# Plain products for the first pair of n-tiles, a casting load for the second weight quad, and new places for the w_down pieces in a fused GeGLU MLP

## Chip, cores and metric

One core of one Trainium2 chip. The metric is device time in microseconds (us) of one launch, median over runs of the same kernel. Engines in the profile: PE is TensorE's matmuls, PEld its weight loads, DVE VectorE, ACT ScalarE, POOL GpSimd, SP the engine that issues plain DMA; a name with a q behind it (SPq, POOLq) is its queue of DMA issues.

## The reference

```python
x: (8, 1024, 1024) fp32;  w_gate, w_up: (1024, 4096);  w_down: (4096, 1024)
gate = x @ w_gate
up   = x @ w_up
gate = 0.5 * gate * (1 + tanh(sqrt(2/pi) * (gate + 0.044715 * gate**3)))
out  = (gate * up) @ w_down
```

## The kernel before

The kernel works through 8192 tokens in eight passes of 1024, all operands in fp16, with accumulation in fp32. In each pass "gate_up" makes h and "down" multiplies it by w_down. Gate_up of passes 0 to 2 takes 16 pairs of 128-wide n-tiles (gate and up weights of both), each pair by a seven-product (Strassen-Winograd) scheme: 14 product steps of 4 matmuls of 512 columns. Operands of five of the products are sums of token blocks (`sum_x`) or of weight blocks (`sum_w`), made by VectorE. Two pairs share a weight quad: 512 columns of both weights, in one of two ring slots. Quads come by a load from GpSimd's queue that casts fp32 to fp16. Pass 0 also has to fetch and transpose its own tokens, and to make w_down's operands, which all later passes read back.

```python
def x0_rest():                      # second half of tokens and of the first weight columns: pair 0, after step 4
    for g in range(G):
        x0_cast(1, g)               # DVE, fp32 -> fp16
    for kh in range(2):
        for w in range(2):
            cast_first(w, kh, slice(256, 512))      # ACT
    used = [ps_free[g] for g in range(G)]
    for g in range(G):
        x0_transpose(1, g)          # PE, then copies by DVE and ACT
    write_banks(used)               # identity matmuls
    ...                             # sum_w and sum_x in turns

# start of the kernel: transposes of the first token half, then
write_banks(range(8))               # eight identity matmuls, 512 columns
for kh in range(2):
    for w in range(2):
        cast_first(w, kh, slice(0, 256))

# in gate_up_one, pass 0
first = p == 0 and i == 0
if first:
    at(4, x0_rest)
for u in range(8 if q == 0 else 0):         # second quad: staged in fp32, cast by ACT in eight pieces
    s = (5, 8, 11, 14, 16, 18, 20, 22)[u]
    if s // 14 == e:
        k = s % 14 + 1
        at(k, cast_stage, 8 + u)
        at(k, load_stage, 8 + u + 4)
...
if e == 1:
    at(13, load_raw, p, q + 2)              # next quad by casting DMA, step 13 of an odd pair
for n in range(4):                          # four batches of w_down
    s0 = 36 * n + 34                        # product step, counted through pass 0
    for ds, f, a in (
        (0, wd_load, (n, 0)), (2, wd_load, (n, 1)), (4, wd_load, (n, 2)), (6, wd_load, (n, 3)),
        (14, wd_sums, (0,)), (15, wd_sums, (1,)), (16, wd_sums, (2,)), (17, wd_sums, (3,)),
        (19, wd_store, (n,)),
    ):
        pr, k = divmod(s0 + ds - 1, 14)
        if pr == i:
            at(k + 1, f, *a)                # wd_load: casting DMA; wd_sums: DVE; wd_store: SP

# in down(p): transposes of the next pass's tokens by DMA
if v == (2 if p < FAST - 1 else 0):
    transpose_x(p + 1)
```

## Time and profile before

| | |
|---|---|
| median of 3 runs | 2315.16 us (2313.58 to 2316.32) |
| span of the profiled run | 2316.7 us (its time, 2318.57, lies above all three) |
| TensorE busy | 2282.1 us, 99% |
| VectorE, ScalarE, GpSimd busy | 58%, 42%, 29% |

A timeline line reads: start, length in us, engine, kernel line, operation, what it writes and reads, how many in a row, and in brackets how long the engine had been idle before it and what ended that. In the view of waits: total us, how often, the longest. The prediction shows the lines.

To compare kernels stage by stage I also counted matmul records. No record seems to be missing in these traces (14,668 before, 14,696 after: 28 more, as the code says), so the n-th matmul from the end is the same one in each. That gives the start of each pair and of each down to 0.01 us. Pairs are numbered from 0, so the second pair is pair 1. An undisturbed pair takes 12.09 us, an undisturbed down 96.69 us.

### The profile page before, as it was taken

To read this page: it belongs to the slowest core of one execution; us is meant where nothing else is said; L and a number is where in the kernel's file an instruction comes from. 1 tells how busy PE (TensorE), PEld (TensorE's weight loads), DVE (VectorE), ACT (ScalarE), POOL (GpSimd) and SP (SyncE) were. 2 spreads that over 40 slices of the span, in tenths; PEclk is the share of its full clock that TensorE was granted. 3 is DMA by queue.
4 is the path that set the end of the run, shared out by engine and by line. 5 is a ranking of instruction groups with operands and counts; after the bars stand their busy time and mean duration, and the time that the engine had idled before them with its cause. 6 is when DMAs were issued, how large, how long until landed. Compare 5 with 4: busy or idle time off the path is not lost.

```text
span 2316.7 us, 38115 instructions
## 1 busy us (share of the span) xinstructions
PE 2282.1 (99%) x14668; PEld 1435.2 (62%) x14668; DVE 1350.2 (58%) x1951; ACT 969.9 (42%) x1874; POOL 671.3 (29%) x817
## 2 busy tenths in 40 slices
PE   6989999999999999999999999999999999999999
PEld 3434444444444444888458884688747886488854
DVE  4655547884377862666536673466734667356650
ACT  5434116552155521565125551355414553055520
POOL 1333003330033300454105450145402543034520
PEclk9999999999999999999999999999999999999999
DMA  6978988889799886898779886798857988588762
GB/s 220 188 139 174 254 229 204 203 233 287 188 214 225 210 292 214 272 321 276 219 239 296 300 275 203 257 312 279 278 192 265 316 280 263 194 278 276 268 215 109
DMA packets 258149, 559.28 MB, mean 241 GB/s; under 512 B 74864, under 2 KB 132208, under 8 KB 243824
## 3 DMA queue, kind: packets, MB, share of 16 engines
q1 hardware_dynamic: 204992, 483.46, 61.9%
q0 software_dynamic: 50800, 69.21, 18.1%
q10 hardware_dynamic: 2176, 4.19, 0.5%
q8 instruction: 114, 1.87, 0.3%
q14 instruction: 67, 0.55, 0.1%
HBM read 512.75 MB, written 113.25 MB: 270 GB/s over the span
## 4 chain that ended last, share of the span: by engine, by line
PE 91%; DMA 3%; DVE 2%; SPq 2%; ACT 1%; issue 1%; POOL 0%; ACTq 0%; DVEq 0%; POOLq 0%
PE ps L713 39%; PE ps L825 32%; PE ps L496 20%; SPq L177 1%; DMA ring<-in_w_up_dram 1%; DVE ring L295 1%; DVE tmp L515 1%; DVE x_sums L200 1%; DMA h_a<-in_w_up_dram 0%; DMA ring<-wd_ops 0%; DMA h_a<-in_w_gate_dram 0%; DVE h_a L533 0%; DMA h_s<-in_w_down_dram 0%; ACT ring L260 0%; ACT tmp L507 0%
## 5 line engine op out<-in xcount | busy, mean ns | idle before, releaser
L713 PEld LDWEIGHTS <-ring 128*128 128x128 f16 x8320 | 814.1, 98 | 95.2
L690 POOL TENSOR_TENSOR h_a<-tmp 128x256 f16<-128x256 f32 x640 | 465.3, 747 | 927.4 <-ACT tmp L678 893.5
L713 PE MATMUL ps<-x_sums,ring 128*128 128x256 f16 x5760 | 655.8, 273 | 0.0
L825 PE MATMUL ps<-ring,h_a 128*128 128x512 f16 x2944 | 638.3, 379 | 1.7 <-DMA ring<-wd_ops 1.7
L675 DVE TENSOR_TENSOR tmp<-tmp,ps 128x512 f32<-128x512 f32 x640 | 413.9, 683 | 219.4 <-PE ps L713 166.2
L825 PEld LDWEIGHTS <-h_a 128*128 128x128 f16 x3072 | 300.5, 98 | 363.3 <-DVE tmp L768 2.2
L496 PEld LDWEIGHTS <-ring 128*128 128x128 f16 x2688 | 264.2, 98 | 339.8 <-issue 25.8
L660 ACT COPY tmp<-ps 128x512 f32<-128x512 f32 x520 | 304.4, 585 | 203.4 <-PE ps L713 125.7
L496 PE MATMUL ps<-x_sums,ring 128*128 128x512 f16 x1536 | 355.0, 384 | 13.2 <-DVE h_a L533 5.9
L678 ACT ACTIVATE tmp<-tmp 128x256 f32<-128x256 f32 x640 | 263.7, 417 | 173.3 <-DVE tmp L673 80.5
L764 ACT ACTIVATE tmp<-ps 128x512 f32<-128x512 f32 x128 | 76.4, 597 | 589.1 <-PE ps L825 589.1
L713 PE MATMUL ps<-x_b,ring 128*128 128x256 f16 x2560 | 305.6, 273 | 0.0
L522 POOL TENSOR_TENSOR h_a<-tmp 128x512 f16<-128x512 f32 x96 | 147.6, 1538 | 431.4 <-ACT tmp L520 350.5
L496 PE MATMUL ps<-x_b,ring 128*128 128x512 f16 x1152 | 265.0, 379 | 1.7 <-ACT ps L512 0.9
L673 DVE TENSOR_TENSOR tmp<-ps,tmp 128x512 f32<-128x512 f32 x240 | 165.5, 689 | 152.2 <-ACT tmp L660 104.8
L768 DVE SCALAR_TENSOR_TENSOR tmp<-ps,tmp 128x512 f32<-128x512 f32 x64 | 44.2, 691 | 305.3 <-ACT tmp L764 260.3
L515 DVE TENSOR_TENSOR tmp<-ps,tmp 128x512 f32<-128x512 f32 x192 | 129.6, 684 | 133.7 <-ACT tmp L507 131.2
L507 ACT COPY tmp<-ps 128x512 f32<-128x512 f32 x192 | 112.4, 586 | 97.2 <-PE ps L496 89.5
L772 DVE TENSOR_TENSOR h_a<-h_a,h_a 128x2048 f16<-128x2048 f16 x96 | 111.2, 1215 | 58.3 <-PE ps L825 58.3
L295 DVE TENSOR_TENSOR ring<-ring 128x1024 f16<-128x1024 f16 x192 | 136.0, 722 | 11.1 <-DMA ring<-in_w_up_dram 7.0
L520 ACT ACTIVATE tmp<-tmp 128x512 f32<-128x512 f32 x96 | 60.1, 626 | 157.9 <-DVE tmp L515 157.9
L825 PE MATMUL ps<-ring,h_s 128*128 128x512 f16 x480 | 104.9, 379 | 0.0
(63 smaller groups left out, 784.8 us busy)
## 6 DMA issues: line engine op xcount, KB each, us to landing
ring<-w_ops SPq DMA_DIRECT2D x480, 512.0 KB, 4.6
ring<-wd_ops SPq DMA_DIRECT2D x105, 1024.0 KB, 5.2
out_dram<-tmp SPq DMA_DIRECT2D x128, 256.0 KB, 3.0
w_ops<-x_sums SPq DMA_DIRECT2D x110, 256.0 KB, 6.2
ring<-in_w_gate_dram POOLq DMA_DIRECT2D x22, 1024.0 KB, 10.0
ring<-in_w_up_dram POOLq DMA_DIRECT2D x22, 1024.0 KB, 17.6
w_ops<-h_s SPq DMA_DIRECT2D x82, 256.0 KB, 4.8
x_half<-in_x_dram POOLq DMA_DIRECT2D x7, 2048.0 KB, 15.5
```

The costliest lines, as they stand in the source:

```text
L295: nc.vector.tensor_tensor(o, a, b, op)
L496: nc.tensor.matmul(ps(b, w), lhs[:, k], rhs[:, k, :], start=(first and k == 0), stop=(k == KH - 1), skip_group_check=True,)
L507: nc.scalar.copy(tl((n, w)), ps("a", w))
L515: nc.vector.tensor_tensor(o, ps("b", w), o, ADD)
L522: nc.gpsimd.tensor_tensor(hq[TO[n]][:, i, :], tmp[:, t[n, 1]], tmp[:, t[n, 0]], MUL)
L660: nc.scalar.copy(tmp[:, t[o[1]]], ps_all[:, bank[o[2]]])
L673: nc.vector.tensor_tensor(d, b, a, SUB)
L675: nc.vector.tensor_tensor(d, a, b, ADD if o[4] == "add" else SUB)
L678: nc.scalar.activation(d, d, GELU, scale=GSC)
L690: nc.gpsimd.tensor_tensor(h, tmp[:, t[o[1]], MQ : 2 * MQ], g, MUL)
L713: nc.tensor.matmul(ps_all[:, bank[c], w * MQ : (w + 1) * MQ], lhs[:, w, k], rhs[:, k], start=(first and w == 0 and k == 0), stop=(k == KH ...
L825: nc.tensor.matmul(ps_all[:, bank[b, g]], lhs[:, j, g * P : (g + 1) * P], dc[:, n, :], start=(first and j == 0), stop=(j == NP - 1), skip_ ...
```

## The change

Intent: start the array earlier. Pair 0 is done by eight plain products, ordered so that the first half of tokens and the first weight columns are enough for the first 32 matmuls, and half of K for the first 16 of them. The second quad comes by casting DMA, released once half of the second-column casts are done (a one-column GpSimd copy into `mark` waits for the cast). The w_down batches get places such that no quad is issued between their pieces. The removal of the staging helpers, and of `write_banks` and `x0_rest`, is cut here.

```diff
+            if p == 0 and i == 0:
+                first_pair()
+                continue
             if p == 0:
-                for u in range(8 if q == 0 else 0):
-                    ...                                  # eight cast_stage / load_stage
                 if e == 1:
                     at(13, load_raw, p, q + 2)
...
-                    s0 = 36 * n + 34
+                    s0 = 28 * n + 59
...
-                        (14, wd_sums, (0,)), (15, wd_sums, (1,)),
-                        (16, wd_sums, (2,)), (17, wd_sums, (3,)), (19, wd_store, (n,)),
+                        (16, wd_sums, (0,)), (17, wd_sums, (1,)),
+                        (18, wd_sums, (2,)), (19, wd_sums, (3,)), (21, wd_store, (n,)),
...
-            pair(p, i, extra, SEQ0 if first else SEQ, AFTER0 if first else AFTER1)
+            second = p == 0 and i == 1
+            pair(p, i, extra, SEQ0 if second else SEQ, AFTER0 if second else AFTER1)
...
+    def first_pair():
+        ...                     # products(mh, kh, c): tokens mh, K half kh, token columns c; outputs: gelu, mul
+        for g in range(G):
+            x0_cast(0, g)
+        for g in range(G):
+            x0_transpose(0, g)
+        for kh in range(2):
+            for w in range(2):
+                cast_first(w, kh, slice(0, 256))
+        take(0)
+        for kh in range(2):
+            products(0, kh, slice(0, MH))
+        for g in range(2):
+            x0_cast(1, g)
+        for g in range(2):
+            x0_transpose(1, g)
+        outputs(0, 0)
+        outputs(0, 1)
+        for g in range(2, G):
+            x0_cast(1, g)
+        take(1)
+        for kh in range(2):
+            products(1, kh, slice(0, MQ))
+        for g in range(2, G):
+            x0_transpose(1, g)
+        ...                     # order of free PSUM banks
+        for n, (kh, w) in enumerate(((0, 0), (0, 1), (1, 0), (1, 1))):
+            cast_first(w, kh, slice(256, 512))
+            if n == 1:
+                nc.gpsimd.tensor_copy(mark, raw(0, 0)[:, w, kh * KH, 256:257])
+                load_raw(0, 1)
+        for kh in range(2):
+            products(1, kh, slice(MQ, MH))
+        sum_x(1)
+        ...                     # sums of the second pair, outputs(1, 0), outputs(1, 1)
```

More of the change, by code (lines that the diff above doesn't have):

```diff
@@ L143 @@
     identity = const.tile([P, P], FP16, name="identity")
+    mark = const.tile([P, 1], FP16, name="mark")
     xq = {
@@ L239, in ssum @@
         return rg[:, o : o + 4096].rearrange("p (s w k n) -> p s w k n", s=4, w=2, k=KH)
-    def staging(u):
-        o = 8192 + (u % 4) * 2048
-        return xc[:, o : o + 2048].bitcast(FP32).rearrange("p (k n) -> p k n", k=2)
-    def eighth(u):
-        q, e = divmod(u, 8)
-        k, w = divmod(e, 2)
-        return q, w, slice(2 * k, 2 * k + 2)
-    def load_stage(u):
-        q, w, k = eighth(u)
-        if q == 1:
-            nc.scalar.dma_start(
-                out=staging(u), in_=w_v[w][:, k, q * 512 : (q + 1) * 512]
-            )
-    def cast_stage(u):
-        q, w, k = eighth(u)
-        nc.scalar.copy(raw(0, q)[:, w, k], staging(u))
     def staging0(w, kh):
@@ L553, in at @@
                 extra[k].append(lambda: f(*a))
-            first = p == 0 and i == 0
-            if first:
-                at(4, x0_rest)
+            if p == 0 and i == 0:
+                first_pair()
+                continue
             if p == 0:
-                for u in range(8 if q == 0 else 0):
-                    s = (5, 8, 11, 14, 16, 18, 20, 22)[u]
-                    if s // 14 == e:
-                        k = s % 14 + 1
-                        at(k, cast_stage, 8 + u)
-                        at(k, load_stage, 8 + u + 4)
-                if first:
-                    for u in range(8, 12):
-                        at(5, load_stage, u)
                 if e == 1:
@@ L593, in gate_up_one @@
                 at(13, load_raw, p, q + 2)
-            ks = (6, 8, 10, 12) if first else (3, 5, 7, 9) if e == 0 else (11, 12, 13, 14)
+            ks = (3, 5, 7, 9) if e == 0 else (11, 12, 13, 14)
             for n, k in enumerate(ks):
@@ L898, in down, with products, outputs, take @@
         order[0] = order[0][2:] + order[0][:2]
-    def write_banks(banks):
-        for b in banks:
-            nc.tensor.matmul(
-                ps_all[:, b], identity, x0_f16[:, 0, 0:MH],
-                start=True, stop=True, skip_group_check=True,
-            )
-    def x0_rest():
+    def first_pair():
+        bank = {}
+        def products(mh, kh, c):
+            for w in range(2):
+                for j in range(2):
+                    for k in range(KH):
+                        nc.tensor.matmul(
+                            ps_all[:, bank[mh, j, w], c],
+                            raw(0, 0)[:, w, kh * KH + k, j * P : (j + 1) * P],
+                            xq[f"b{kh + 1}{mh + 1}"][:, k, c],
+                            start=(kh == 0 and k == 0 and c.start == 0),
+                            stop=(kh == 1 and k == KH - 1),
+                            skip_group_check=True,
+                        )
+        def outputs(mh, j):
+            t = tmp_free.popleft()
+            g, u = bank[mh, j, 0], bank[mh, j, 1]
+            nc.scalar.activation(tmp[:, t], ps_all[:, g], GELU, scale=GSC)
+            nc.vector.tensor_tensor(
+                hq[f"a{mh + 1}{j + 1}"][:, 0, :], ps_all[:, u], tmp[:, t], MUL
+            )
+            tmp_free.append(t)
+            ps_free.extend((g, u))
+        def take(mh):
+            for j in range(2):
+                for w in range(2):
+                    bank[mh, j, w] = ps_free.popleft()
@@ L909, in x0_rest @@
         for g in range(G):
-            x0_cast(1, g)
+            x0_cast(0, g)
+        for g in range(G):
+            x0_transpose(0, g)
         for kh in range(2):
             for w in range(2):
-                cast_first(w, kh, slice(256, 512))
-        used = [ps_free[g] for g in range(G)]
-        for g in range(G):
-            x0_transpose(1, g)
-        write_banks(used)
-        for k in range(2):
-            sum_w(0, 0, k)
-            sum_x(k + 1)
-        for k in range(2):
-            sum_w(0, 0, k + 2)
-            sum_x(k + 3)
+                cast_first(w, kh, slice(0, 256))
@@ new lines, in first_pair @@
+        take(0)
[4 more added lines that the diff above has]
+        for g in range(2):
+            x0_transpose(1, g)
+        outputs(0, 0)
[7 more added lines that the diff above has]
+            x0_transpose(1, g)
+        b = list(ps_free)
+        ps_free.clear()
@@ new lines, in first_pair @@
+        ps_free.extend((b[2], b[0], b[3], b[1]))
+        for n, (kh, w) in enumerate(((0, 0), (0, 1), (1, 0), (1, 1))):
[6 more added lines that the diff above has]
+        sum_x(1)
+        sum_w(0, 1, 0)
+        sum_w(0, 1, 1)
+        sum_x(2)
+        outputs(1, 0)
+        outputs(1, 1)
@@ L925 @@
+        sum_x(3)
+        sum_w(0, 1, 2)
+        sum_w(0, 1, 3)
+        sum_x(4)
     for g in range(G):
@@ L933 @@
                 x0_load(1, g)
-    for g in range(G):
-        x0_cast(0, g)
-    for g in range(G):
-        x0_transpose(0, g)
-    write_banks(range(8))
-    for kh in range(2):
-        for w in range(2):
-            cast_first(w, kh, slice(0, 256))
     for p in range(NPASS):
```

## The prediction

> **What bounds the kernel now.** I read the page first, then all waits of TensorE, then the chain that ended last, then the instructions in order of time at the two places where TensorE stood still. The page:
>
> ```profile
> span 2316.7 us, 38115 instructions
> PE 2282.1 (99%) x14668; PEld 1435.2 (62%) x14668; DVE 1350.2 (58%) x1951; ACT 969.9 (42%) x1874; POOL 671.3 (29%) x817
> PE   6989999999999999999999999999999999999999
> ```
>
> TensorE is the bound: 99% busy, with its only weak slices at the start (57.9 us each). At most 2316.7 - 2282.1 = 34.6 us of idle can be won without removing matmuls. All waits of TensorE over the whole run:
>
> ```profile
> PE ps L903 <- ACT x_b L229: 7.5, 1, 7.5
> PE ps L226 <- DVE h_a L219: 6.8, 6, 5.1
> PE ps L496 <- DVE h_a L533: 5.9, 1, 5.9
> PE ps L496 <- ACT ps L512: 3.2, 5, 1.1
> PE ps L496 <- ACT tmp L507: 2.3, 2, 1.4
> ```
>
> The first, second and fifth, and the first idle of the fourth (0.9), lie in the first pair of n-tiles (before 43 us). The third is one hole at 143 us. The change aims at exactly these. The hole, in the chain that ended last (start, us, what):
>
> ```profile
> 130.02 7.54 DMA h_s<-in_w_down_dram
> 137.56 8.53 issue
> 146.09 0.13 DVE h_s L356
> ```
>
> and in order of time on VectorE and TensorE:
>
> ```profile
> 130.02 0.59 POOL L338 DMA_DIRECT2D h_s<-in_w_down_dram  x1
> 146.09 0.69 DVE L356 TENSOR_TENSOR h_s<-h_s 128x1024 f16<-128x1024 f16 x1 [8.54 <-issue]
> 148.64 1.87 PE L496 MATMUL ps<-x_sums,ring 128*128 128x512 f16 x4 [5.87 <-DVE h_a L533]
> 151.58 6.63 PE L496 MATMUL ps<-x_sums,ring 128*128 128x512 f16 x20 [1.08 <-ACT ps L512]
> ```
>
> The last w_down piece of the third batch is issued at 130.02, just behind the two casting transfers of a weight quad (128.26 and 129.15). It takes 16.0 us to land, where its three predecessors took 4 to 5. VectorE, in order, sits on the sum that needs it; the products behind it wait; PSUM isn't freed; TensorE stops for 5.87 + 1.08 us. Afterwards 24 matmuls take 1.87 + 6.63 = 8.50 us; at the usual 0.216 us each they take 5.18. Together 10.3 us. Check: the same matmul group of two successive pairs starts at 123.61, 135.70 and then 158.05; a pair is 12.09, so 22.35 is 10.26 late.
>
> The start, in order of time:
>
> ```profile
> 9.98 3.27 PE L903 MATMUL ps<-h_a,identity 128*128 128x512 f16 x8
> 13.09 1.89 PE L496 MATMUL ps<-x_b,ring 128*128 128x512 f16 x8
> 26.66 1.04 ACT L273 CAST ring<-h_a 128x1024 f16<-128x1024 f32 x1 [1.68 <-DMA h_a<-in_w_up_dram]
> 28.24 2.05 PE L903 MATMUL ps<-h_a,identity 128*128 128x512 f16 x4 [7.45 <-ACT x_b L229]
> 53.33 4.48 PE L496 MATMUL ps<-x_b,ring 128*128 128x512 f16 x20
> ```
>
> After 16 matmuls of the first pair (P1, P2) nothing more can be done until the second half of tokens is transposed, which on ScalarE stands behind casts of the second weight columns; the last waits for its load until 26.66. Then half-speed matmuls and ScalarE's eight second-quad casts. Counting 56 matmuls per pair, the second pair begins at 43.07 and the third at 53.33 + 12 x 0.216 = 55.92. With 14 pairs at 12.10 (169.3) and the 10.3 hole the pass should end at 235.5; the chain puts down's first matmul at 235.91. So the sum closes.
>
> **What the Trainium skill says.** (1) "TensorE: Matmul & The Clock Gate", Part 1: an idle array runs at half clock, and gets the full one after about 3.4 us of sustained work in a free-running window. The trace agrees: matmuls of 0.427 us in the 4.8 us after 28.24 and until 156.1, at a granted clock of 0.50; 0.216 otherwise. (2) "DMA: Bandwidth & Descriptors", SWDGE vs HWDGE: a load that casts can only be issued from GpSimd, and only one such queue is allocated. The trace fits: a small casting load behind a quad waits for it. (3) Same page, Anatomy of one DMA: about 2 us + bytes/436e3. For 2 MiB read that is 6.8 us; the trace has 8.5 and 13.2 for the gate and up halves issued at 54.40 and 55.48, and I use those. (4) "PSUM — Partial Sum Buffer", The four PSUM rules: bits that say "written" are set by TensorE only. I read the identity matmuls as setting them before ScalarE seeds a bank; plain products set them too. No run shows this yet.
>
> **The change part by part.**
>
> *a. Plain products for pair 0.* Removed: 56 half-output products, 12 identity matmuls (3.27 + 2.05 us, but partly beside waits). Added: 2 token halves x 2 K halves x 2 weights x 2 tiles x 4 = 32 matmuls of 512 columns and 64 of 256, i.e. 64 full ones: 8 more than before, 1.73 us. What is gained is order: 32 of them need only the first tokens and first weight columns. Working forward with durations of the trace:
> - The first cast ends at 12.3 (11.26 + 1.04), the fourth at 15.3. TensorE starts at 12.4, cold, as nothing warms it. I take 5 us at 0.427 (12 matmuls) and 20 at 0.216: to 21.8. The loads don't bind it.
> - 16 transposes (1.06) to 22.9, their ScalarE copies to 23.5; 32 matmuls of 256 columns (3.5) to 27.0.
> - ScalarE: table load 1.28, two GELUs to 25.9; VectorE: two h products to 26.6, then the last two token casts to 27.9. So transposes end at 28.4, copies at 29.0.
> - ScalarE's four second-column casts (all landed by 26.6) run 29.0 to 33.0. The last 32 short matmuls (3.5) read the same tiles; a load into the other columns of a staging tile already waits for the former one in this trace (12.78, for the landing at 12.77), so I let the casts pace them: to 33.9.
> - The second pair, in the order P1, P2, P5...: 33.9 + 12.1 = 46.0. VectorE supplies its operands from 33.0: two weight sums (0.6), one x sum (1.2), two products (1.3), x sum (1.2), two weight sums, x sum (1.2): t2 at 35.5, t3 at 38.0, t4 at 40.4; the matmuls that need them come at about 38, 41 and 42.5. It fits.
>
> *b. Second quad by casting DMA.* Removed: eight ScalarE casts (8 x 1.04 us) and 4 MB of loads from ScalarE's queue. Added: one tiny GpSimd copy and the quad's two loads, held until the second cast (31.0). Issues at 31.3 and 32.3; landing + 8.5 and + 13.2: 39.8 and 45.5. The sums for pair 2 need both, and stand on VectorE after step 10 of pair 1, at about 43. They hold it to 46; the third pair's third product group wants its operand at 48.6 and gets it at about 48.5. I allow 0.5: third pair at an effective 46.5.
> Gain of a and b: 55.92 + 0.2 (a wait on VectorE at 58.87) - 46.5 = 9.6 us.
>
> *c. w_down pieces ahead of quads.* Each batch now has its four pieces at steps 3 to 9 of an even pair, sums at steps 5 to 8 of the odd one, and the next quad at its step 13; no quad is issued between pieces. The first batch of before had nearly this place: issued at 60.5 and 66.7 behind a quad of 54.4, sums waited 3.3 and 0.6 us and ran at 72.54 and 73.82, with no wait of TensorE. From the pair's start (55.92) that is 16.6 and 17.9; the new slots are at 12.1 + 4 x 0.864 = 15.6. VectorE would wait some 1.6 us four times, over before the accumulation in step 13. I credit the whole hole: 10.3 us.
>
> Sum: 9.6 + 10.3 = 19.9. The forward pass leaves out semaphore delays and smaller waits, and these only add; 1.7 us for them. 2315.2 - 18.2 = **2297 us**. Passes 1 to 7 have no changed instruction.
>
> **Rivals.**
> - *The quad's load becomes the new wait.* It starts at 31 instead of the staged loads' 26.7, and its second half has no reserve. Against: the queue is empty then. If up takes 17.6 us (median of the run), pair 2 starts 4 to 5 us later: 2301.
> - *The cold clock eats the start.* No identity matmuls warm the array. For: the windows are free-running, so 3.4 to 6.8 us cold; short pauses at 23, 27 and 28 could fail a window. Costs 1 to 4 us: up to 2301.
> - *The hole moves.* Every batch now lands 16 to 18 us after its pair's start, behind a quad, and four of them could each cost TensorE 1 to 2 us: 2301 to 2305. The first batch of before speaks against it.
> - *Start hidden by a later limit.* If down of pass 0 waited on transfers bound to absolute time, gains would be returned. Its only DMA wait is 1.7 us, and its transfers are issued relative to matmuls; unlikely. All lost: 2315.
> - *Better than thought:* a warm array at once and no pacing: 2291.
>
> **Range and chances.** Start gain 5 to 12, hole 7 to 10.5 with both rarely at an end: 2290 to 2304. Over 2% faster needs 2269, a gain of 46 us, more than all idle time (34.6): 1%. 2% slower needs a new hole of 46 us: 1%.
>
> **What would show it.** The waits of TensorE lose the 7.5 on L229's copies and the 5.9 on the h product; no hole near 130 to 150. First plain matmuls near 12.4 at 0.427 us, half speed for 3 to 7 us; second pair at 34, third near 46, down's first matmul near 217 (235.9 before). The quad's up half lands near 45. Wrong would be: third pair after 50, a wait on h products in an odd pair, or a wait in down that was not there.

## The result

The changed kernel: 2300.39 us median of 4 runs (2299.53 to 2304.98); the kernel before in the same comparison 2315.59 us (2313.58 to 2316.32). Ratio 0.994, 95% interval 0.9923 to 0.9957. A ratio here is the mean time of one kernel's runs over that of the other's runs of the same rounds, so it isn't quite the ratio of the medians quoted. The gain is 15.2 us where 18.2 were predicted; the time lies in the predicted range. Its size is less sure than that looks: when the changed kernel was timed again (experiment 11) the ratio was 0.9922, some 18 us. The profiled run happens to be the slowest of the four; a likely reason is told below.

The page of the changed kernel, the lines that answer to those of before:

```profile
span 2303.0 us, 38141 instructions
PE 2277.2 (99%) x14696; PEld 1436.5 (62%) x14696; DVE 1348.0 (59%) x1945; ACT 958.4 (42%) x1860; POOL 670.1 (29%) x818
PE   7999999999999999999999999999999999999999
```

Only the first slice is weak now. All waits of TensorE over the run:

```profile
PE ps L476 <- DVE tmp L495: 7.1, 5, 2.4
PE ps L227 <- DVE h_a L220: 6.8, 5, 5.1
PE ps L795 <- DMA ring<-wd_ops: 3.9, 1, 3.9
PE ps L879 <- ACT ring L253: 2.3, 1, 2.3
PE ps L879 <- DVE x_b L229: 1.1, 2, 0.6
PE ps L476 <- ACT ps L492: 0.5, 1, 0.5
```

The two big ones are gone: 7.5 us on ScalarE's token copies and 5.9 on the h product. The 6.8 us on token casts, of which 5.1 lie before the first token has landed, are as before, though the prediction lists them among what the change aims at. New is 7.1 us, in five pieces, on VectorE's accumulations (line 495), and the wait for a w_down chunk in down has grown from 1.7 to 3.9. The start, in order of time on several engines:

```profile
12.38 9.95 PE L879 MATMUL ps<-x_b,ring 128*128 128x512 f16 x32 [2.32 <-ACT ring L253]
...
28.31 1.22 PE L227 MATMUL ps<-identity,h_a 128*128 128x128 f16 x16 [0.85 <-DVE h_a L220]
...
32.68 1.08 POOL L260 DMA_DIRECT2D ring<-in_w_gate_dram  x1
...
33.53 1.89 PE L476 MATMUL ps<-x_b,ring 128*128 128x512 f16 x8
33.76 0.90 POOL L260 DMA_DIRECT2D ring<-in_w_up_dram  x1
...
46.69 0.69 DVE L275 TENSOR_TENSOR ring<-ring 128x1024 f16<-128x1024 f16 x1 [2.36 <-DMA ring<-in_w_up_dram]
...
50.97 4.48 PE L476 MATMUL ps<-x_sums,ring 128*128 128x512 f16 x20 [1.92 <-DVE tmp L495]
```

TensorE starts its first product at 12.38 and the second pair at 33.53 (43.07 before). But the second quad is released only at 32.68, its up half lands at 46.7, VectorE stands 2.36 us waiting for it, and TensorE then 1.92 us in the third pair. The fourth batch of w_down pieces, on VectorE, GpSimd and TensorE:

```profile
165.49 0.69 DVE L334 TENSOR_TENSOR h_s<-h_s 128x1024 f16<-128x1024 f16 x1 [5.84 <-DMA h_s<-in_w_down_dram]
...
170.07 1.26 POOL L502 TENSOR_TENSOR h_a<-tmp 128x512 f16<-128x512 f32 x1 [8.31 <-DVE tmp L495]
...
174.89 1.45 PE L476 MATMUL ps<-x_sums,ring 128*128 128x512 f16 x6 [1.29 <-DVE tmp L495]
```

VectorE waits 5.84 us for pieces. GpSimd waits for VectorE's accumulation, and only after that, at 171.29, issues the next quad. 9 us after VectorE's wait TensorE waits 1.29 for VectorE. In down of pass 0, the queue of plain DMA and TensorE:

```profile
250.59 30.89 SPq L178 DMA_TRANSPOSE x_b<-x_half  x4
...
293.81 6.38 PE L795 MATMUL ps<-ring,h_a 128*128 128x512 f16 x21 [3.93 <-DMA ring<-wd_ops]
```

Four DMA transposes hold that queue for 30.89 us (28.41 before). The load of the sixth product's chunk stands behind them, and after 3.93 us of idle the array also runs at half clock for a while (matmuls 0.43 us apart from 294.7 to 298.1).

The stages, worked out from the starts of matmuls in the two profiles (us):

| stage | before | after | difference |
|---|---|---|---|
| up to the second pair | 43.07 | 33.53 | -9.54 |
| second pair | 12.85 | 12.74 | -0.11 |
| third pair | 12.44 | 14.20 | +1.76 |
| pairs 3 to 7 | 60.43 | 60.43 | 0.00 |
| pairs 8 and 9 | 34.44 | 24.35 | -10.09 |
| pairs 10 to 13 | 48.35 | 51.22 | +2.87 |
| pairs 14 and 15 | 24.17 | 24.17 | 0.00 |
| down, pass 0 | 98.57 | 102.47 | +3.90 |
| gate_up of passes 1 and 2 | 393.44 | 390.95 | -2.49 |
| all that is later, to the last matmul | 1584.91 | 1584.90 | -0.01 |

Up to down the change is worth 15.11 us in this pair of profiles. What comes later isn't shown to be its effect: gate_up of passes 1 and 2 varies by 1.6 and 2.5 us between the profiles of any of these kernels, and down of pass 0 by more. The 15.11 us have a spread too. Three profiles with the old start and places (before, before again, experiment 9) start down at 234.80 to 235.75, three with the new ones (changed, changed again, experiment 8) at 218.43 to 220.64: 14.2 to 17.3 us.

### The profile page after: what moved, and what is told of

It is laid out like the page before. It is cut to its first block, busy times and chain, and to the rows that moved or that the text cites. A ratio compares the mean times of both kernels' runs of the same rounds, so it can differ in the third digit from the quotient of the medians.

```text
span 2303.0 us, 38141 instructions
## 1 busy us (share of the span) xinstructions
PE 2277.2 (99%) x14696; PEld 1436.5 (62%) x14696; DVE 1348.0 (59%) x1945; ACT 958.4 (42%) x1860; POOL 670.1 (29%) x818
## 4 chain that ended last, share of the span: by engine, by line
PE 90%; DMA 5%; DVE 3%; issue 1%; ACT 1%; POOL 0%; SPq 0%; POOLq 0%; DVEq 0%; ACTq 0%
PE ps L683 39%; PE ps L795 33%; PE ps L476 17%; DMA ring<-in_w_up_dram 2%; DMA h_s<-in_w_down_dram 2%; DVE ring L275 1%; DVE tmp L495 1%; DMA ring<-wd_ops 0%; PE ps L879 0%; DMA w_ops<-x_sums 0%; DVE h_a L513 0%; DMA h_a<-in_x_dram 0%; DVE x_sums L201 0%; POOL h_s L318 0%; ACT ring L253 0%
## 5 line engine op out<-in xcount | busy, mean ns | idle before, releaser
L476 PE MATMUL ps<-x_sums,ring 128*128 128x512 f16 x1504 | 341.4, 379 | 7.5 <-DVE tmp L495 7.1
L476 PE MATMUL ps<-x_b,ring 128*128 128x512 f16 x1128 | 259.5, 379 | 0.5 <-ACT ps L492 0.5
## 6 DMA issues: line engine op xcount, KB each, us to landing
ring<-in_w_up_dram POOLq DMA_DIRECT2D x23, 1024.0 KB, 18.4
x_half<-in_x_dram POOLq DMA_DIRECT2D x7, 2048.0 KB, 15.4
```

Source lines behind the costliest of these rows:

```text
L476: nc.tensor.matmul(ps(b, w), lhs[:, k], rhs[:, k, :], start=(first and k == 0), stop=(k == KH - 1), skip_group_check=True,)
```

## The experiments

Twelve runs were made, in three calls, each call on another chip. The kernel before was timed along: 2320.47 us median (2314.14 to 2325.46) in the first, 2322.05 (2314.43 to 2326.70) in the second, 2319.19 (2314.17 to 2325.09) in the third. That spread is wider than in the first comparison, so effects of 2 or 3 us are read from the stages of a trace, and the times only support them. The changed kernel itself was timed along in the third alone (ratio 0.9922, 0.9905 to 0.9939); the intervals of experiments 4 to 8 overlap with this one, so none of those five is told apart from the changed kernel by its time. All kernels were correct.

**1. The new start alone**

```diff
 # changed kernel
-                    s0 = 28 * n + 59
+                    s0 = 36 * n + 34       # and ds 14 to 17, 19 for sums and store, as before
```

> The changed kernel with the old places of the w_down pieces, so only the new start (plain first pair, casting load of the second quad). Theory A (the two parts act in different places and add): the start is as in the changed kernel, third pair effective at about 48.2 us (55.9 before); the hole of TensorE on the h product, 5 to 7 us idle and some 3 us of half clock, is back some 8 us earlier, near 135 us; first matmul of down near 228; time 2315.6 - 7.9 = about 2307.7 us. Rival B (the hole depends on when transfers happen to fall, and an earlier start moves the piece out from behind the quad): no wait on the h product, time 2298 to 2301 us.

Measured: 2310.27 us (2305.76 to 2312.98), ratio 0.9953 (0.9935 to 0.9972). Second pair at 33.27, third at 46.01, down's first matmul at 227.32. The hole is back:

```profile
137.84 0.69 DVE L336 TENSOR_TENSOR h_s<-h_s 128x1024 f16<-128x1024 f16 x1 [8.91 <-DMA h_s<-in_w_down_dram]
...
140.38 1.86 PE L476 MATMUL ps<-x_sums,ring 128*128 128x512 f16 x4 [6.24 <-DVE h_a L513]
```

Pairs 8 and 9 take 34.63 us, 10.5 over two undisturbed ones. Theory A holds: the hole follows the order of issues, not the clock time, and moving the start by 8.4 us (235.75 to 227.32) leaves it whole.

**2. The new w_down places alone**

```diff
 # kernel before
-                    s0 = 36 * n + 34       # ds 14 to 17, 19
+                    s0 = 28 * n + 59       # ds 16 to 19, 21
```

> The kernel before with only the new places of the w_down pieces. Theory A: third pair at 55.9 us as before; the 5.9 us wait on the h product gone, but waits of 1 to 1.5 us on the accumulation behind a w_down sum in some of the odd pairs 5, 7, 9 and 11, 2 to 4 us in sum, as the changed kernel's trace shows (2.6); first matmul of down near 228.7 (235.9 before); time about 2308.4 us. Rival B: without the late start of the quads nothing waits, the whole 10.3 us are won: 2305.3 us, no wait of TensorE between 60 and 225 us.

Measured: 2310.72 us (2308.26 to 2315.82), ratio 0.9961 (0.9944 to 0.9978). Down's first matmul at 230.66; the first two pairs happened to take 1.6 us longer than in the first profile of the kernel before (third pair at 57.51), so from there on 6.7 us are won (173.15 to down's start, against 179.83). Pairs 8 to 13 lose 3.6 us against undisturbed ones; the largest of the waits:

```profile
159.75 4.48 PE L496 MATMUL ps<-x_sums,ring 128*128 128x512 f16 x20 [1.30 <-DVE tmp L515]
```

Theory A again: the hole of 10.3 us shrinks to 3.6, and doesn't vanish. The two parts add: 8.4 and 6.7 us, 15.1 together, against 15.11 for the whole change. That they agree so closely is luck, as the start of down scatters by 1 to 2 us between profiles of one kernel.

**3. The casting load alone, first pair as before**

```diff
 # kernel before: no eighths staged; in x0_rest
                 cast_first(w, kh, slice(256, 512))
+                if (kh, w) == (0, 1):
+                    nc.gpsimd.tensor_copy(mark, raw(0, 0)[:, w, kh * KH, 256:257])
+                    load_raw(0, 1)
```

> The kernel before with only the second quad by casting loads (issued after the second cast of the second columns, about 23.6 us), the first pair still by seven products. ScalarE loses eight casts of about 1 us, several of them in the chain between 34 and 54 us. Theory A (ScalarE's casts held the first two pairs): third pair 3 to 5 us earlier, near 52; hole unchanged in size; time 2311 to 2313 us. Rival B (the first pair is bound by its late token half, the casts lie beside it): within 1 us of before, 2314.5 to 2316.5 us. Rival C (the casting load takes bandwidth from the last column load, which lands later than 26.6): slower start, 2316 to 2320 us.

Measured: 2319.65 us (2310.75 to 2322.53), ratio 0.9993 (0.9974 to 1.0013): no difference by time. In the trace the second pair starts at 41.27 (43.07), the third at 53.35 (55.92), down at 233.21 (235.75): 2.5 us earlier, the sign of theory A at somewhat less than the size I gave (the third pair of the kernel before starts at 55.35 to 55.92 in three profiles, so 2.0 to 2.6). The last column cast begins at 26.75 against 26.66, so theory C falls. So the casting load alone makes some 2.5 of the start's 8.4 us; the larger part needs the plain products.

**4. The changed kernel with its second quad cast by ScalarE**

```diff
 # changed kernel, first_pair and second pair
-                nc.gpsimd.tensor_copy(mark, raw(0, 0)[:, w, kh * KH, 256:257])
-                load_raw(0, 1)
+        for u in range(8, 12):
+            load_stage(u)
+                for u in range(8 if i == 1 else 0):
+                    k = (2, 3, 4, 5, 7, 8, 10, 11)[u]
+                    at(k, cast_stage, 8 + u)
+                    at(k, load_stage, 8 + u + 4)
```

> The changed kernel with the second quad staged in fp32 and cast by ScalarE in eight pieces inside the second pair, as the kernel before did, in place of the casting load. Theory A (ScalarE is too full: eight casts of 1 us beside some 7 us of its own in a pair of 12.7 us): the second pair stretches by 2 to 4 us, third pair effective at 50 to 52 us, time 2302 to 2304.5 us. Rival B (the casting load's late second half, 1.9 us of wait in the changed kernel, is worse than the casts): third pair effective at 46.5 to 48, time 2298.5 to 2300.5 us.

Measured: 2303.29 us (2301.10 to 2309.78), ratio 0.9932 (0.9914 to 0.9950). The second pair takes 16.14 us (12.74), the third 13.95, so the third starts at 48.47 and ends at 62.42 (46.27 and 60.47). ScalarE's copies are what TensorE waits for:

```profile
41.67 1.89 PE L497 MATMUL ps<-x_sums,ring 128*128 128x512 f16 x8 [1.62 <-ACT tmp L508]
```

A second such wait, of 1.46 us, ends at 45.02. Theory A by the trace. The time can't say it: its ratio is level with the changed kernel's, perhaps because in this profile VectorE waited less for w_down pieces (15.6 us in sum, against 19.4) and TensorE lost almost nothing there (0.15 us against 3.06).

**5. The second quad released earlier**

```diff
-            if n == 1:
-                nc.gpsimd.tensor_copy(mark, raw(0, 0)[:, w, kh * KH, 256:257])
+            if n == 0:
+                nc.gpsimd.tensor_copy(mark, staging0(1, 1)[:, 0, 256:257])   # waits for the last staged load
                 load_raw(0, 1)
```

> The changed kernel with the second quad's casting loads released by the landing of the last staged column load (about 26.6 us) in place of the second cast (32.6 us). Theory A (the 1.9 us wait of TensorE in the third pair is the up half of this quad landing at 46.7): it lands near 41, VectorE's weight sums for the third pair no longer wait, the 1.9 us wait is gone, first matmul of down near 218.8 (220.8), time about 2 us less than the changed kernel, 2298.5 us. Rival B (VectorE itself is the limit in the second pair: five sums, four accumulations and products in a row): the wait of VectorE on the load goes, but TensorE still waits 1 us or more; gain 0 to 0.8 us.

Measured: 2300.84 us (2296.23 to 2305.50), ratio 0.9919 (0.9899 to 0.9939).

```profile
25.42 0.19 POOL L934 CAST mark<-h_a 128x1 f16<-128x1 f32 x1 [24.11 <-DMA h_a<-in_w_up_dram]
...
26.62 0.97 POOL L260 DMA_DIRECT2D ring<-in_w_up_dram  x1
...
44.32 0.68 DVE L275 TENSOR_TENSOR ring<-ring 128x1024 f16<-128x1024 f16 x1
```

The up half is issued 7.1 us earlier and lands 12.5 us later, at 39.1. VectorE's weight sum at 44.32 waits for nothing, and the second and third pair take 12.10 and 12.09 us (12.74 and 14.20). Theory A; the 1.92 us wait was this load, and rival B is out. The second pair's 0.64 us aren't its doing: experiment 12 has the early load too, and 12.74 us there. In this run the second pair began later (34.25 against 33.53), since waits of 1.15 and 0.35 us before 28.2 were followed by half clock from 28.9 to 32.3, and the last 32 short matmuls took 5.1 us in place of 3.7. So down starts only 2.15 us earlier than in the changed kernel's profile, and the time doesn't show the expected 2 us.

**6. The w_down pieces between two quads**

```diff
-                    s0 = 28 * n + 59       # ds 16 to 19, 21
+                    s0 = 28 * n + 70       # ds 14 to 17, 19
```

> The changed kernel with each batch of w_down pieces 11 product steps later (last step of an even pair to step 6 of the odd one, sums around the end of the odd pair), so after the former quad has landed and ahead of the next. Theory A (what is left of the hole, 2.6 us in two waits plus small ones, is pieces queued behind the former quad): pieces land 4 to 6 us after issue instead of 11.9 in the median, VectorE waits under 1 us for them, TensorE has no wait between 60 and 218 us; first matmul of down near 217.7 to 218.2; time about 2297.5 us. Rival B (the sums now fall beside the four weight sums at the end of an odd pair, and VectorE becomes late for the next pair): new waits of 1 us or more on accumulations or h products; no gain, 2300 to 2303 us.

Measured: 2297.86 us (2294.54 to 2302.22), ratio 0.9906 (0.9887 to 0.9926). No wait of TensorE is left between 52 and 216 us, none of VectorE on a piece; pairs 3 to 15 take 157.1 us, 12.09 each (160.2 in the changed kernel). Down starts at 216.44. The sixteen pieces land 6.9 us after issue in the median (12.3 in the changed kernel): longer than the 4 to 6 I expected, but early enough. Theory A.

**7. A warm array for the first product**

```diff
+        for b in range(6):
+            nc.tensor.matmul(ps_all[:, 4 + b % 4], identity, x0_f16[:, 0, 0:MH],
+                             start=True, stop=True, skip_group_check=True)
         take(0)
         for kh in range(2):
             products(0, kh, slice(0, MH))
```

> The changed kernel with six matmuls on the identity, whose results are overwritten, in the idle 2.3 us before the first plain product, to start TensorE's clock earlier. Theory A (the first 14 products ran at half clock, 0.427 us each, until 18.3 us, because nothing warmed the array): full clock from about 12.7 us, the first 32 products end near 19.5 to 20.5 (22.3), everything to the third pair 2 us earlier; time about 2298.4 us. Rival B (the second columns of the weights, which land until 26.6 us, or the chain of token copies and GELU set the second pair): the first products end earlier, the second pair starts at 33 to 33.5 as before; time 2300 to 2301 us.

Measured: 2298.02 us (2294.27 to 2301.69), ratio 0.9906 (0.9887 to 0.9924).

```profile
9.80 2.75 PE L911 MATMUL ps<-h_a,identity 128*128 128x512 f16 x6
12.36 7.09 PE L879 MATMUL ps<-x_b,ring 128*128 128x512 f16 x32
```

The same 32 products take 7.09 us in place of 9.95, and the second pair starts at 30.66, 2.9 us earlier than in the changed kernel's first profile. Theory A. That profile had one of the longest cold stretches: in the seven profiles of the unwarmed start the full clock came 2.9 to 6.0 us after the first product, the 32 products took 8.5 to 10.0 us, and the second pair started at 32.33 to 34.25, 33.2 in the mean. With the six matmuls it starts at 30.66 here and 30.79 in experiment 12. So warming is worth some 2.5 us in the mean, 1.5 to 3.6 from profile to profile. The removed identity matmuls had a side use that the change gave up: they warmed the array.

**8. The DMA transposes of down queued earlier, in the changed kernel**

```diff
+                    if p == 0 and v == 1 and nb == 1 and g == 0:
+                        transpose_x(1)
...
-                        if v == (2 if p < FAST - 1 else 0):
+                        if p and v == (2 if p < FAST - 1 else 0):
```

> The changed kernel with the DMA transposes of the next tokens in down of pass 0 queued at the second half of the second product (about 21 us after down's start) in place of the start of the third (28 us). They hold the queue 28 to 31 us, and the load of the weight chunk for the sixth product stands behind them: TensorE waited 1.7 us for it before, 3.9 in the changed kernel's profile, where its clock then was halved for 4 us. Theory A: the load is issued 5 to 7 us earlier, no wait of TensorE in down of pass 0, and the spread between runs (2299.5 to 2305.0) shrinks, for it came from this wait: 1.7 to 4 us less, 2296.5 to 2298.5 us. Rival B (the load's slot comes free no earlier, or the transposes then hold stores and temporary tiles): the wait stays or moves to ScalarE's copies; time 2300 to 2304 us.

Measured: 2298.49 us (2296.65 to 2300.47), ratio 0.9907 (0.9888 to 0.9927). Down of pass 0 takes 96.70 us, nothing waits, and the spread of six runs is 3.8 us. The transposes hold the queue for 25.90 us only, and at 26.11 in experiment 2's profile the wait was gone without this edit. But the load is issued 52.9 us after down's start here, against 58.2 to 62.7 with the transposes at their old place, and lands 4.3 us before its product. By this run theory A holds; the next one limits it.

**9. The same in the kernel before**

The edit is that of experiment 8, made in the kernel before.

> The kernel before with only the earlier DMA transposes in down of pass 0. Theory A (the wait there is no part of the change: it belongs to both kernels and spreads the times of both): down of pass 0 takes 96.7 us, the spread of times shrinks to under 5 us where the kernel before had 2314 to 2327 on these chips, and the median is 2 to 7 us below the kernel before of the same rounds. Rival B (the wait was made longer by the change, the kernel before hardly has it): gain 0 to 2 us, spread as before.

Measured: 2316.37 us (2315.19 to 2325.97), ratio 0.9998 (0.9978 to 1.0019). Four runs lie between 2315.2 and 2316.6, two at 2323.6 and 2326.0. The profiled one is the slowest; first its queue of plain DMA, then its longest wait of TensorE:

```profile
256.21 38.51 SPq L177 DMA_TRANSPOSE x_b<-x_half  x4
```

```profile
PE ps L825 <- DMA ring<-wd_ops: 7.8, 1, 7.8
```

The transposes, issued earlier, took 38.51 us, and down 106.45. Theory A fails: the edit makes no reliable gain, and it can make the wait worse. Rival B's numbers came true (no gain, spread as before), but not its reason: experiment 10 finds the wait in the kernel before too. While the transposes were under way the two casting loads of the next pass's first quad landed 18.4 and 21.7 us after issue, against 15.4 and 10.0 in the good run of experiment 8. Which of the two kinds of transfer slows the other, and why it goes one way or the other from run to run, stays open.

**10. The kernel before once more**

Nothing edited.

> The kernel before unchanged, for a second profile of its down of pass 0. Theory A (that wait spreads over runs of both kernels): 98 to 104 us there, the hole at 143 us again (pairs 8 and 9 together 34.4 us), third pair at 55.5 to 57.5. Rival B: 98.6 again within 0.3, as the wait is short and steady in this kernel.

Measured: one look, 2320.57 us (state unknown). The hole is there (pairs 8 and 9: 34.05 us), the third pair starts at 55.36, and down of pass 0 takes 102.64 us, after transposes of 30.85. Theory A: the kernel before has this spread too. All profiles of the unchanged transposes in one table:

| kernel of the profile | transposes hold the queue, us | down of pass 0, us |
|---|---|---|
| new w_down places alone | 26.11 | 96.75 |
| staged second quad | 28.09 | 97.99 |
| before, first profile | 28.41 | 98.57 |
| casting load alone | 28.61 | 98.93 |
| early second quad | 28.75 | 98.66 |
| changed, second profile | 29.18 | 101.63 |
| new start alone | 29.50 | 101.73 |
| warm array | 29.62 | 102.06 |
| before, second profile | 30.85 | 102.64 |
| changed, first profile | 30.89 | 102.47 |
| late pieces | 31.37 | 104.29 |

Down grows with the transposes' time by and large, and jumps by 2.7 us or more between the first five rows and the others. TensorE's wait is 2.1 us at most in the former, with no half clock after it, and 3.2 us at least in the latter, all with half clock after it (matmuls 0.43 us apart for 3.4 us in the changed kernel's first profile). Kernels of both families stand at both ends. So the 3.9 us that the changed kernel's first profile lost in down are not shown to be an effect of the change.

**11. The changed kernel once more, beside experiments 9 and 12**

Nothing edited.

> The changed kernel unchanged, on the chip and in the rounds of the others, for a second profile and as the base of comparison. Theory A: pairs as in its first profile within 0.6 us from the second pair's start on (third to fourth pair 14.2, pairs 8 to 13 3.1 us over 12.1 each); down of pass 0 anywhere between 97 and 104 us, as the DMA transposes fall; time 2299 to 2305 us. Rival B (the waits of its first profile were one bad run): no waits behind w_down sums, down at 98.6 as before.

Measured: 2301.93 us (2297.11 to 2304.02), ratio 0.9922 (0.9905 to 0.9939). Second pair at 33.59, third at 46.32 and 14.18 us long, pairs 8 to 13 1.7 us over undisturbed ones, where the first profile had 3.1. The first two are the same within 0.06 us; the loss behind w_down sums is there again, but its size varies more than the 0.6 us that I allowed. Rival B falls all the same.

**12. All four edits together**

> The changed kernel with all four edits together: second quad released by the last staged landing, w_down pieces 11 steps later, six warming matmuls, earlier DMA transposes in down of pass 0. Theory A (each removes its own wait of TensorE and they add): from the traces of the single edits against the changed kernel: third to fourth pair 12.1 (14.2), pairs 3 to 15 at 12.1 each (3.1 less), first pair's end near 30.7 (33.5), down of pass 0 at 96.7 (102.5 in that profile, about 98.5 in a typical run): first matmul of down near 213 (220.8); time about 2291 to 2292.5 us, TensorE idle only at the start, before 31 us. Rival B (with the start faster the quad's load is late again, or the edits hide each other): the third pair waits 1 us or more, 2294 to 2297 us.

Measured: 2292.09 us (2290.77 to 2302.41), ratio 0.9897 (0.9874 to 0.9919), where the changed kernel has 0.9922 in the same rounds. Second pair at 30.79, the third 12.09 long, down at 212.75 (220.64), down 96.69. Waits of TensorE from the start to 310 us:

```profile
PE ps L227 <- DVE h_a L220: 6.7, 5, 5.1
PE ps L881 <- DVE x_b L229: 1.1, 2, 0.6
PE ps L476 <- ACT ps L492: 0.5, 1, 0.5
```

Theory A: the edits add, and the version beats both kernels in the median (the interval overlaps a little with the changed kernel's, 0.9905 to 0.9939). Four runs lie between 2290.8 and 2292.5; two, at 2299.4 and 2302.4, have the look of experiment 9's slow ones. No profile of them was taken, so that they too are slow transposes is likely, not shown.

## Why the prediction was right, and where its steps were off

The range held the time, and the two mechanisms were right: the start and the hole act in different places and add (experiments 1 and 2). By the first comparison the sum was too large by 3 us; the later ratio of some 18 us is level with it, but part of that is scatter of stages that the change doesn't touch. Its terms, from the first profiles:

| step | predicted | measured (first profile) |
|---|---|---|
| first plain product | 12.4 us, cold for 5 us | 12.38, cold for 5.9 (2.9 to 6.0 over seven profiles) |
| end of the first 32 | 21.8 | 22.33 |
| second pair | 33.9 | 33.53 |
| third pair | 46.0, then 0.5 of wait | 46.27, then 1.92 of wait |
| quad's up half lands | 45.5 | 46.7 |
| gain of the start | 9.6 | 7.9 (7.3 to 9.2 over the six profiles named above) |
| gain of the hole | 10.3 | 7.2 (6.8 to 8.6) |
| allowance for smaller waits | -1.7 | not a term of its own |
| whole | 18.2 | 15.2 (median), 15.1 up to down |

- *Forward pass through the first pair.* Right within 0.6 us, since the lengths came from the trace of before; that the cold stretch was so near the 5 us taken is luck, as it changes from run to run. It also assumed that the last short matmuls are paced by the casts; that was not so: they ran at 0.11 us each (30.04 to 33.5) beside casts that ended at 34.4. Later copies and later casts made up for it.
- *The quad's load as a new wait.* A rival of the prediction, given 4 to 5 us if slow and 0.5 in the sum. It was 1.92, because the second cast ended at 32.5, not 31.0. Experiment 5 shows the cause by removing it.
- *"I credit the whole hole."* This is the step that failed. It took the first batch of the kernel before as a model: VectorE waiting 1.6 us four times, with no effect on TensorE. Measured waits were 3.2, 4.6, 5.8 and 5.8 us. In the first batch the piece that is waited for landed 16.2 us after its pair's start, about as the model had it (16.6), but VectorE came to the sum 13.0 us after that start, not 15.6. The first batch has no stores of a former batch ahead of it; from the second on, the next quad's up half lands 14.4 to 15.0 us after issue, not 13.2, and each delay makes GpSimd issue the next quad later: 1.65 us ahead of the even pair that follows, then 0.83, then 0.41 behind its start. That the stores cause the longer landings is argued from the order in time, not tested. In this profile VectorE's waits of 3.2 and 4.6 us cost TensorE 0.2 us at most, those of 5.8 about 1.4 each. The prediction's rival "the hole moves" named this, at 1 to 2 us per batch in all four. Experiment 6 shows it by putting the pieces where no quad is ahead of them.
- *The cold clock.* Counted in the sum, and about right. Experiment 7 shows what it was worth: 2.9 us against the first profile, some 2.5 in the mean. The 3.4 to 6.8 us of cold time in the prediction's rival are an estimate, one to two of the windows that its point 1 cites; seven profiles show 2.9 to 6.0. The rival's other half, that short pauses near 27 and 28 us halve the clock again, came true in one profile, that of experiment 5.
- *The ceiling.* The prediction took the 34.6 us of idle time for all that can be won. A busy array at half clock counts as busy: of the hole's 10.3 us, 3.3 are such time.
- *The identity matmuls.* That plain products can take their place ahead of ScalarE's writes to PSUM was a reading that no run had shown (point 4 of the prediction); the changed kernel does without them and gave correct results.
- *Later limits.* Nothing from the change was given back in later passes. But I took the 1.7 us wait in down for a fixed figure; over eleven profiles with the transposes in their old place down of pass 0 took 96.75 to 104.29 us.

## What to carry to other kernels

When a wait behind a queue is removed by moving an issue, count what will be ahead of the transfer at its new place, with the bandwidth of that moment, and don't take the one instance that had nothing ahead of it for the rule. Before dropping filler work from the bound engine, ask what it did besides, and look for instructions of double length right after the place where it stood. Where runs spread by more than the effect, compare the starts of the same instruction in the traces, stage by stage: many stages that weren't touched agree to 0.01 us, and those that don't show how large the scatter is.

## What the Trainium skill lacked or had wrong

- "TensorE: Matmul & The Clock Gate", Part 1 and Part 4: full clock after about 3.4 us of sustained work, with transposes not counting. From the first 512-column matmul to the full clock it took 1.6 to 3.6 us in the seven profiles where such matmuls follow the transposes without a break (9.98 to 12.62 in the kernel before, 9.80 to 12.40 in experiment 7), and 2.9 to 6.0 us in the seven where 2.3 us of idle lie between. So the transposes seem to count for something here; no run was made to test it.
- The same part's caution about clock records: the part doesn't say that records can be absent at the start of a trace. The first record of the changed kernel's trace begins at 18.22 us, at full clock. Before it there is none, and the view counts that time as a clock of 1.00, while 14 matmuls of 512 columns took 5.90 us there, 0.42 each. Where there are records they agree with the lengths, as at 294.7 to 298.1.
- "DMA: Bandwidth & Descriptors", Anatomy of one DMA: 2 us + bytes/436e3 gives 6.8 us for 2 MiB read. A casting load of that size landed 8.7 us after issue and its follower, issued 0.9 us behind it, after 12.9 (changed kernel, 46.3 us on), and after 14.4 to 15.0 in later batches. The page has no figure for a load that casts.
- The same page, "DMA Transpose (X-bar)" and the latency table (261 GB/s): four transposes of 512 KiB each held the queue 25.9 to 38.5 us, from experiment 8's run to experiment 9's, while casting loads were under way. That is an estimate of 81 down to 54 GB/s, 2 MiB over the time that they held it. No page tells of this spread.
